# A decoder step whose first conditioning columns become features straight from fp32 weights

## The chip, the cores and the metric

The kernel runs on one core of a Trainium2 chip as a single program. The metric is the device time of one execution in microseconds (us); times of several executions are given by their median. TensorE (PE in the profile) multiplies matrices, and its weight loads stand apart as PEld. VectorE is DVE, ScalarE is ACT, GpSimd is POOL, and SyncE (SP) issues the transfers.

## What is computed

One layer of a hybrid decoder, for a prompt of 2048 tokens and for 64 sample tokens (8 sequences of 8), all in fp32. The part that matters here is its entry:

```python
ada = silu(c) @ w_ada + b_ada                    # c: 1 prompt row and 8 sample rows, w_ada: 1024 x 6144
sh_m, sc_m, g_m, sh_f, sc_f, g_f = split(ada, 6) # 1024 columns each
h = rmsnorm(x, norm_mix) * (1 + sc_m) + sh_m
proj = h @ w_in                                  # 1024 x 3584
# then retention and stick-breaking attention, w_out, and a gated MLP with a short convolution
```

Each of the six parts is a shift, a scale or a gate, and differs by row: row 0 of the nine conditioning rows belongs to the prompt, rows 1 to 8 to the eight sample sequences.

## The kernel before

An fp32 product is made from two fp32r numbers, high and low: `split` (line 173) copies the high part on ACT and subtracts for the low part on DVE, and three matmuls (`mm3`, lines 295 to 297) or, with a short left side, two, give the product. Weights arrive as `raw` tiles of 1 MB and are split into `whl` tiles, of which the pool has six buffers, that is three pairs.

The head (from line 1425) is all that runs before the first projection. It needs `coef[0]` (scale) and `coef[1]` (shift), which hold for each of the 1024 features the nine values of the conditioning rows, and `xT`, the first 512 prompt tokens and the 64 sample tokens, normalized and turned so that features lie on partitions. `modulate` (line 587) makes `acts` from both: `acts[0]` holds features 0 to 511, `acts[1]` the rest. Scale and shift are four blocks of 512 columns of `w_ada`: block 2 and block 0 are scale and shift of the lower half of the features, block 3 and block 1 those of the upper half.

- `prep` (line 466) applies silu to the nine rows and turns them into `s18`, high and low side by side.
- `ada` (line 505) takes a block: 2 MB in two loads, four splits, and sixteen matmuls at line 516, with `s18` as the weights and 512 columns of `w_ada` moving. The result, 18 rows of 512 columns, goes through ACT to `ar` (line 521), the bias is loaded into row 18, and four fp32 matmuls with the constant `fold` (line 551) add the high part, the low part and the bias and turn the columns onto partitions. DVE writes `coef` from there (lines 558 and 562).
- `raw_features` (line 569) does five tiles of x, four of 128 prompt rows and one of 64 sample rows: load, sum of squares on ACT (line 384), a short chain on POOL, scaling on DVE (line 576), eight PE transposes (line 580), and two evacuations to `xT`, one on DVE and one on ACT (line 584).
- `vectors` (line 477) loads small vectors as rows and turns them with one transpose (line 490).

The pool for the head holds three buffers for x, four for `raw`, and two for `ar`. A load that needs a buffer in use waits in SP's queue, and all that follows it in that queue waits with it. A scheduler orders each engine's instructions from the program's order; every engine then runs its own list strictly in order. After the head, `modulate` and the first two split column blocks of `w_in` let the projection begin: the matmuls of lines 295 to 297 on `d` and `z` with `act` and `whl`.

Of the kernel before, what the change touches and what calls it, by code (L numbers as in the profile page):

```python
# [5 lines left out]
F32 = mybir.dt.float32  # L6
# [3 lines left out]
ALU = mybir.AluOpType  # L10
# [3 lines left out]
P = 128  # L14
D = 1024
KT = D // P
SEQ = 2048
NB = 4
TB = SEQ // NB
NT = TB // P  # L20
DB = 8
DS = 8
NS = DB * DS
# [124 lines left out]
def body(tc, I, O):  # L148
    nc = tc.nc
    pe, dve, act, pool, sp = nc.tensor, nc.vector, nc.scalar, nc.gpsimd, nc.sync  # L150
# [3 lines left out]
    def T(pl, shape, dt, tag):  # L154
        count[0] += 1
        return pl.tile(shape, dt, tag=tag, name=f"{tag}_{count[0]}")

    def tt(eng, o, a, b, op):
        eng.tensor_tensor(o, a, b, op)  # L159
# [7 lines left out]
    def ld(o, i):  # L167
        dma(sp, o, i)
# [4 lines left out]
    def split(hi, lo, src, eng=dve):  # L173
        act.copy(hi, src)  # L174
        tt(eng, lo, src, f(hi), ALU.subtract)
# [83 lines left out]
    def pd():  # L259
        return T(psd, [P, 512], F32, "d")  # L260
# [17 lines left out]
    def w_rows(src, r0, n, c0, pl=None):  # L278
        for r in range(r0, r0 + n, 4):
            m = min(4, r0 + n - r)  # L280
            raw = T(pl or wraw, [P, 2048], F32, "raw").rearrange("p (a b) -> p a b", a=4)
            ld(
                raw[:, :m],
                src[r * P : (r + m) * P, c0 : c0 + 512].rearrange("(k p) c -> p k c", p=P),
            )
            yield r - r0, raw[:, :m]
# [179 lines left out]
    def prep(pl, kp):  # L466
        sg = T(pl, [P, D], F32, "hj")[:9]
        act.activation(sg, c9, AF.Sigmoid)
        tt(dve, c9, c9, sg, ALU.mult)
        ps = pz()  # L470
        for k in range(KT):
            pe.transpose(ps[:, k * 16 : k * 16 + 9], c9[:, k * P : (k + 1) * P], ident[:9, :9])
        s18 = T(kp, [P, KT, 18], F32R, "s18")
        split(s18[:, :, 0:9], s18[:, :, 9:18], ps[:, : KT * 16].rearrange("p (k s) -> p k s", s=16)[:, :, 0:9])
        return s18

    def vectors(pl):
        rows = T(pl, [108, P], F32, "vrows")
        for nme, o, n in (
            ("norm_mix", V_NM, 8), ("norm_ffn", V_NF, 8), ("conv_w", V_CW, 66),  # L480
            ("conv_b", V_CB, 22), ("sb_gn", V_SG, 4),
        ):
            src = I[nme][0]
            if nme == "conv_w":
                src = src.rearrange("j (a p) -> (j a) p", p=P)
            else:
                src = src.rearrange("(a p) -> a p", p=P)
            ld(rows[o : o + n, :], src)
        ps = pz()
        pe.transpose(ps[:, :108], rows, ident[:108, :108])  # L490
        dve.tensor_copy(vecs, ps[:, :108])

    def state_rows(pl):
        ps = pz()
# [71 lines left out]
            yield 0.9  # L566


    def raw_features(hp, xT):

        for i, o, n in TILES + [(NT, TB, NS)]:
            x = T(hp, [P, D], F32, "hx")
            ld(x[:n], xp[o : o + n, :] if i < NT else xs)
            junk = T(hp, [P, D], F32, "hj")
            r = row_rstd(x, [junk[:, :512], junk[:, 512:]], n)
            dve.tensor_scalar(x[:n], x[:n], r[:n, 0:1], None, ALU.mult)
            for kh in range(2):
                ps = pz()
                for k in range(4):
                    pe.transpose(  # L580
                        ps[:, k * n : (k + 1) * n], x[:n, (kh * 4 + k) * P : (kh * 4 + k + 1) * P], ident[:n, :n]
                    )
                src = ps[:, : 4 * n].rearrange("p (k t) -> p k t", k=4)
                (act.copy if kh else dve.tensor_copy)(xT[:, kh * 4 : kh * 4 + 4, o : o + n], src)
            yield
# [831 lines left out]
    def chain(*gens):  # L1417
        for g in gens:
            yield from g
# [3 lines left out]
    with tile_pool("in1", 2) as ip0:  # L1423
        ip = _Bufs(ip0, dict(xt=2, rot=1, hf=3, st=2, kf=2, vst=1, ar=1, s18=1, gnm=1))
        with tile_pool("head", 2) as hp0:
            hp = _Bufs(hp0, dict(hx=3, hj=1, xT=1, vrows=1, raw=4, ar=2))
            first = {2: list(w_rows(I["w_ada"][0], 0, KT, 1024, hp))}
            s18 = prep(hp, ip)
            xT = T(hp, [P, KT, TB + NS], F32, "xT")
            feats = raw_features(hp, xT)  # L1430
            vectors(hp)
            for n, _ in enumerate(ada(hp, s18, (2, 0, 3), first)):
                if n:
                    next(feats, None)
            for _ in ada(hp, s18, (1,), first):
                pass
            first_in[0, 0, SQ] = list(w_fm(w_in, SQ))
            modulate(xT, coef[0], coef[1], acts, range(4))
            modulate(xT, coef[0], coef[1], acts, range(4, 8))
            bb = T(cp, [P, HS], F32, "bb")  # L1440
            ld(bb, I["sb_bias"][0].partition_broadcast(P))
            nb = T(cp, [P, HS], F32, "nb")
            dve.tensor_scalar(nb, bb, -1.0, None, ALU.mult)
            sel4 = T(cp, [4, P], F32R, "sel4")
            dve.tensor_copy(sel4, cc("sel4", 4))
            gnm.append(T(ip, [P, 512], F32, "gnm"))
            ld(gnm[0], I["ret_gn"][0].partition_broadcast(P))
            state_rows(hp)
        c9_cm.__exit__(None, None, None)
        with tile_pool("dec", 2) as dp0:  # L1450
            dp = _Bufs(
                dp0,
                dict(smp=1, page=3, khl=2, vhl=3, aT=10, qsm=1, ksm=1, oT=1,
                     tm=1, sbsq=1, dm=1, dmh=1, ptab=1, sbc=1, dbias=1, m8n=1),
            )
            smp = T(dp, [P, KT, 2, NS], F32R, "smp")
            for kh in range(2):
                pool.tensor_copy(smp[:, kh * 4 : kh * 4 + 4], f(acts[kh][:, :, :, TB:]))
            ins = _Stream(
                chain(*[in_block(g, ip, smp) for g in range(NB)]), 650.0  # L1460
            )
            rest = _Stream(ada(ip, s18, (4, 5, 6, 7, 8, 9, 10, 11)), 60.0)
            side = _Stream(decode(dp), 490.0)
            _weave([ins, side, rest], side)
        with tile_pool("ret", 1) as rp0, tile_pool("att0", 2) as tp0:
            rp = _Bufs(rp0, dict(rmh=3, qT=2, kT=1, rv=2, rg=2, scd=2, km=1, on=3, S=2, bst=4, mv=2, nm=2, va=2))
            tp = _Bufs(tp0, dict(aq=1, abe=6, aom=2, ahl=4, o2=1, sbsq=1))
            ins.total, ins.got = 650.0 - ins.got, 0.0
            _weave([
                ins,  # L1470
                rest,
                _Stream(chain(retention_sample(rp), retention(rp)), 100.0),
                _Stream(attention([0], tp), 60),
            ])
# [92 lines left out]
```

## Time and profile before

| what | us |
|---|---|
| median of 3 runs | 3450.88 |
| lowest and highest of them | 3449.73, 3461.42 |
| the profiled execution | 3453.42 |
| its span, first to last instruction | 3451.7 |
| PE busy in the span | 3287.4 (95%) |
| DVE busy | 2288.9 (66%) |
| ACT busy | 1779.6 (52%) |
| POOL busy | 1018.7 (30%) |

The profile is one execution. In its timeline an entry is a start, a duration, the engine, the source line, the operation, and "out<-in"; instructions of one kind in a row are merged into one entry with their count, whose duration runs from the first start to the last end. An fp32 matmul that isn't a transpose shows as two records on PE. What stands in brackets is the idle time before an entry and what ended it. Where a window's granted clock of TensorE is given, 1.00 is 2.4 GHz and 0.50 is 1.2 GHz.

### The profile page before, as it was taken

How to read it: one execution, taken by the hardware profiler on the slowest of the kernel's cores; microseconds unless marked ns; L12 is line 12 of the kernel's file. 1: busy time of each engine (PE TensorE's matmuls, PEld its weight loads, DVE VectorE, ACT ScalarE, POOL GpSimd, SP SyncE). 2: the span in 40 equal slices, each digit the busy share in tenths (PEclk: the TensorE clock that was granted, in tenths of full speed). 3: DMA queues.
4: the chain of work that ended last, by engine and by line, in shares of the span. 5: the costliest groups of instructions: out<-in, count | busy, mean ns of one | idle time of the engine just before them, and what ended most of it. 6: DMA issues, size and time to landing. Idle time of an engine off the chain costs nothing. (4 is left out here: it accounts for less than half of the span.)

```text
span 3451.7 us, 49588 instructions
## 1 busy us (share of the span) xinstructions
PE 3287.4 (95%) x17111; PEld 2683.8 (78%) x17111; DVE 2288.9 (66%) x3258; ACT 1779.6 (52%) x3153; POOL 1018.7 (30%) x1898
## 2 busy tenths in 40 slices
PE   7998999999999989999998999999899999999998
PEld 5877777776677767877877788777677787799997
DVE  5466666665555567777777787876877775554545
ACT  5457566654544446555556555554655553433223
POOL 3012011101343233434334343333433323321113
PEclk8999999999999999999999999999999999999999
DMA  6766766666756773433454343335333334332221
GB/s 227 232 200 193 231 224 224 220 229 201 212 172 197 242 215 107 123 115 120 122 185 130 107 124 112 118 109 189 110 119 107 115 103 138 119 110 84 80 86 65
DMA packets 406232, 527.71 MB, mean 153 GB/s; under 512 B 27830, under 2 KB 244009, under 8 KB 405982
## 3 DMA queue, kind: packets, MB, share of 16 engines
q1 hardware_dynamic: 405982, 524.55, 48.4%
q8 instruction: 136, 2.23, 0.3%
q14 instruction: 114, 0.93, 0.1%
HBM read 442.47 MB, written 81.99 MB: 152 GB/s over the span
## 5 line engine op out<-in xcount | busy, mean ns | idle before, releaser
L159 DVE TENSOR_TENSOR whl<-raw,whl 128x1024 fp32r<-128x1024 f32 x456 | 572.9, 1260 | 557.5 <-ACT whl L174 552.2
L174 ACT CAST whl<-raw 128x1024 fp32r<-128x1024 f32 x456 | 477.1, 1050 | 901.7 <-PE d L296 636.4
L295 PE MATMUL d<-act,whl 128*128 128x512 f32 (+2 forms) x2016 | 740.3, 368 | 7.8 <-ACT act L424 7.0
L297 PE MATMUL d<-act,whl 128*128 128x512 f32 (+2 forms) x2016 | 736.0, 365 | 4.6 <-DVE whl L159 4.6
L296 PE MATMUL d<-act,whl 128*128 128x512 f32 (+2 forms) x2016 | 733.1, 364 | 3.1 <-POOL act L159 2.2
L295 PEld LDWEIGHTS d<-act,whl 128*128 128x128 f32 x2016 | 384.6, 191 | 67.9 <-ACT act L424 8.7
L297 PEld LDWEIGHTS d<-act,whl 128*128 128x128 f32 x2016 | 384.2, 191 | 64.8 <-DVE whl L159 5.9
L296 PEld LDWEIGHTS d<-act,whl 128*128 128x128 f32 x2016 | 385.4, 191 | 59.8 <-POOL act L159 2.6
L295 PE MATMUL d<-whl,ff 128*128 128x512 f32 x704 | 280.2, 398 | 0.0
L297 PE MATMUL d<-whl,ff 128*128 128x512 f32 x704 | 279.4, 397 | 0.0
L296 PE MATMUL d<-whl,ff 128*128 128x512 f32 x704 | 279.1, 396 | 0.0
L295 PE MATMUL d<-whl,act 128*128 128x512 f32 x640 | 258.0, 407 | 10.4 <-DVE hf L159 9.3
L296 PE MATMUL d<-whl,act 128*128 128x512 f32 x640 | 258.3, 404 | 0.1
L297 PE MATMUL d<-whl,act 128*128 128x512 f32 x640 | 257.1, 402 | 0.0
L1139 DVE TENSOR_TENSOR_SCAN aom<-aom,acy 128x512 f32<-128x512 f32 x192 | 251.6, 1310 | 3.6 <-ACT aom L1125 3.0
L159 DVE TENSOR_TENSOR abe<-abe,aom 128x512 f32<-128x512 f32 (+2 forms) x320 | 232.1, 725 | 27.0 <-POOL abe L1129 5.1
L1163 PE MATMUL acc<-ahl,avv 128*128 128x512 f32 (+3 forms) x640 | 226.4, 413 | 17.6 <-ACT ahl L174 9.9
L1125 ACT ACTIVATE aom<-z,nb 128x512 f32<-128x512 f32 (+2 forms) x320 | 201.4, 629 | 74.6 <-PE z L1122 58.1
L1122 PE MATMUL z<-akk,aq 128*128 128x512 f32 (+3 forms) x640 | 192.9, 377 | 12.0 <-DVE scd L159 5.8
L1126 ACT ACTIVATE abe<-z,bb 128x512 f32<-128x512 f32 (+2 forms) x320 | 200.1, 625 | 0.0
L159 DVE TENSOR_TENSOR ahl<-z,ahl 128x512 fp32r<-128x512 f32 (+1 forms) x320 | 191.4, 598 | 6.7 <-ACT ahl L174 6.4
L159 POOL TENSOR_TENSOR ff<-ff,hf 128x512 f32<-128x512 f32 (+1 forms) x101 | 159.4, 1600 | 105.3 <-DVE hf L159 91.5
(292 smaller groups left out, 6208.8 us busy)
## 6 DMA issues: line engine op xcount, KB each, us to landing
raw<-in_w_in SPq DMA_DIRECT2D x56, 1024.0 KB
raw<-in_w_up_gate SPq DMA_DIRECT2D x44, 1024.0 KB
raw<-in_w_up_val SPq DMA_DIRECT2D x44, 1024.0 KB
akk<-k SPq DMA_DIRECT2D x160, 256.0 KB
page<-in_cache_k_pages SPq DMA_DIRECT2D x128, 256.0 KB
page<-in_cache_v_pages SPq DMA_DIRECT2D x128, 256.0 KB
raw<-in_w_down SPq DMA_DIRECT2D x32, 1024.0 KB
raw<-in_w_ada SPq DMA_DIRECT2D x24, 1024.0 KB
```

The costliest lines, as they stand in the source:

```text
L159: eng.tensor_tensor(o, a, b, op)
L174: act.copy(hi, src)
L295: pe.matmul(ps, sh, mh, start=start, stop=False)
L296: pe.matmul(ps, sh, ml, start=False, stop=False)
L297: pe.matmul(ps, sl, mh, start=False, stop=stop)
L1122: pe.matmul(z[:, :n], qs[g, h][:, i * P : (i + 1) * P], kk[:, c, :n], start=c == 0, stop=c == 1)
L1125: act.activation(om[:, :n], z[:, :n], AF.Sigmoid, bias=nb[:, h : h + 1], scale=-SCALE)
L1126: act.activation(be[:, :n], z[:, :n], AF.Sigmoid, bias=bb[:, h : h + 1], scale=SCALE)
L1139: dve.tensor_tensor_scan(rv, rv, rv, init, ALU.mult, ALU.bypass)
L1163: pe.matmul(accs[0][:, cs], kv[u][1][:, kt, :], m[:, cs], start=(s == g and kt == 0 and c == 0), stop=(s == 0 and kt == NT - 1 and c == 1),)
```

## The change

Blocks 2 and 0 are computed another way, and the order of loads and of PE's work in the head is another. Blocks 3 and 1 keep the old way.

- `prep` also returns `s9`, the turned conditioning rows in plain fp32.
- `ada_features` is new. It takes 128 columns of the unsplit fp32 `raw` tile as the weights and nine columns of `s9` as the moving side, so that the result has features on partitions at once: 32 fp32 matmuls a block, which sum four row tiles each into one of two column groups of a PSUM tile. Two additions on DVE sum the groups and the bias, and a third operation makes the scale. The casts, the subtractions, the copy to `ar` and the `fold` matmuls of the two blocks are gone.
- The bias of all four blocks comes with the small vectors (`bvec`), as 16 more rows of the same transpose.
- All five tiles of x get a buffer of their own and are loaded right behind block 2; block 0 follows. Block 3 is loaded into the two buffers of `wraw`, which the first block of `w_in` uses next. Block 1 takes the buffers that block 2 leaves. `ar` has one buffer instead of two.
- `modulate` of features 0 to 511 is called between blocks 3 and 1.

The core of the diff:

```diff
     def prep(pl, kp):
...
-        split(s18[:, :, 0:9], s18[:, :, 9:18], ps[:, : KT * 16].rearrange("p (k s) -> p k s", s=16)[:, :, 0:9])
-        return s18
+        pv = ps[:, : KT * 16].rearrange("p (k s) -> p k s", s=16)[:, :, 0:9]
+        s9 = T(pl, [P, KT, 9], F32, "s9")
+        dve.tensor_copy(s9, pv)
+        split(s18[:, :, 0:9], s18[:, :, 9:18], s9)
+        return s9, s18
...
+    def ada_features(s9, bvec, j, raws):
+
+        ps = pd()
+        for k0, raw in raws:
+            for q in range(4):
+                o = (k0 + q) * 16
+                for k in range(4):
+                    pe.matmul(
+                        ps[:, o : o + 9], raw[:, k, q * P : (q + 1) * P], s9[:, k0 + k, :],
+                        start=k == 0, stop=k == 3,
+                    )
+            yield
+        kind, half = divmod(j, 2)
+        pv = ps[:, :128].rearrange("p (c q s) -> p c q s", c=2, s=16)[:, :, :, 0:9]
+        wide = lambda a, o: a[:, o : o + 4].unsqueeze(2).to_broadcast([P, 4, 9])
+        c = coef[1 - kind][:, half * 4 : half * 4 + 4, :]
+        tt(dve, c, pv[:, 0], wide(bvec, j * 4), ALU.add)
+        tt(dve, c, c, pv[:, 1], ALU.add)
+        if kind == 1:
+            dve.scalar_tensor_tensor(c, c, 1.0, wide(vecs, V_NM + half * 4), ALU.add, ALU.mult)
...
-            hp = _Bufs(hp0, dict(hx=3, hj=1, xT=1, vrows=1, raw=4, ar=2))
-            first = {2: list(w_rows(I["w_ada"][0], 0, KT, 1024, hp))}
-            s18 = prep(hp, ip)
+            hp = _Bufs(hp0, dict(hx=5, hj=1, xT=1, vrows=1, raw=4, ar=1, s9=1, bvec=1))
+            rows_of = lambda j, pl=hp: list(w_rows(I["w_ada"][0], 0, KT, j * 512, pl))
+            xrows = first_rows(hp)
+            first = {2: rows_of(2)}
+            rows = list(xrows)
+            first[0] = rows_of(0)
+            s9, s18 = prep(hp, ip)
             xT = T(hp, [P, KT, TB + NS], F32, "xT")
-            feats = raw_features(hp, xT)
-            vectors(hp)
-            for n, _ in enumerate(ada(hp, s18, (2, 0, 3), first)):
-                if n:
-                    next(feats, None)
+            bvec = vectors(hp)
+            first[3] = rows_of(3, wraw)
+            feats = raw_features(hp, xT, rows)
+            for _ in chain(ada_features(s9, bvec, 2, first.pop(2)), ada_features(s9, bvec, 0, first.pop(0))):
+                next(feats, None)
+            next(feats, None)
+            first[1] = rows_of(1)
+            for _ in ada(hp, s18, (3,), first):
+                pass
+            modulate(xT, coef[0], coef[1], acts, range(4))
             for _ in ada(hp, s18, (1,), first):
                 pass
             first_in[0, 0, SQ] = list(w_fm(w_in, SQ))
-            modulate(xT, coef[0], coef[1], acts, range(4))
             modulate(xT, coef[0], coef[1], acts, range(4, 8))
```

In the orders below a row is a source line, the operation, "out<-in" with buffer numbers, the shape, and how many such follow each other. PE's list near its end of the head, before the change: block 0's last matmuls (`d_332`), x tiles and `fold` matmuls stand by turns, and block 3 (`d_453`) follows the last x tile (`hx_427`, 64 sample rows).

```order
L516 MATMUL d_332<-whl_386,s_120_226 18x512
L516 MATMUL d_332<-whl_387,s_120_226 18x512
L580 MATMUL z_407<-con_171,hx_394 128x128 x4
L580 MATMUL z_413<-con_171,hx_394 128x128 x4
L551 MATMUL z_421<-con_171,ar_331 128x9 x4
```

PE's list now, from the turning of the conditioning rows on: `d_262` is block 2, `d_344` block 0, the `hx` tiles are the five of x, and `d_453` is block 3.

```order
L472 MATMUL z_231<-con_171,c_105_168 128x9 x8
L508 MATMUL d_262<-s_128_241,raw_210 128x9 x16
L508 MATMUL d_262<-s_128_241,raw_212 128x9 x16
L508 MATMUL d_344<-s_128_241,raw_224 128x9 x16
L508 MATMUL d_344<-s_128_241,raw_226 128x9 x16
L495 MATMUL z_253<-con_171,vrows_246 128x124
L613 MATMUL z_290<-con_171,hx_214 128x128 x4
L613 MATMUL z_296<-con_171,hx_214 128x128 x4
L613 MATMUL z_329<-con_171,hx_216 128x128 x4
```

All transposes of x, which stood between the matmuls of blocks 2 and 0, now stand behind both blocks; three more tiles and then block 3 follow.

DVE's list around the last evacuation of x (`xT_229<-z_440`, 64 sample rows) and block 3's first subtraction (`whl_457`), before:

```order
L584 COPY xT_229<-z_407 128x4x128
L558 COPY coef_108_174<-z_421 128x36
L576 TENSOR_SCALAR hx_427<-hx_427,rs_b_436 64x1024
L593 TENSOR_SCALAR xT_229<-xT_229,coef_107_173,coef_108_174 128x512 x2
L584 COPY xT_229<-z_440 128x4x64
L159 TENSOR_TENSOR whl_457<-raw_454,whl_456 128x1024
L159 TENSOR_TENSOR whl_465<-raw_454,whl_464 128x1024
```

The same place now (`z_436` is the last tile, `whl_455` block 3's first subtraction):

```order
L617 COPY xT_245<-z_372 128x4x128
L617 COPY xT_245<-z_411 128x4x128
L626 TENSOR_SCALAR xT_245<-xT_245,coef_107_173,coef_108_174 128x512
L617 COPY xT_245<-z_436 128x4x64
L159 TENSOR_TENSOR whl_455<-raw_258,whl_454 128x1024
L626 TENSOR_SCALAR xT_245<-xT_245,coef_107_173,coef_108_174 128x512
L159 TENSOR_TENSOR whl_463<-raw_258,whl_462 128x1024
```

Block 3's subtractions still stand behind the last evacuation of x, and one of the two modulating operations has moved behind it too.

SP's list before, from the head's last loads of `w_ada` on (`ar_498` is the bias of block 1):

```order
L165 DMA raw_500<-in_w_ada 128x4x512
L165 DMA raw_518<-in_w_ada 128x4x512
L165 DMA ar_498<-in_b_ada 1x512
L165 DMA raw_544<-in_w_in 128x8x256
L165 DMA bb_594<-in_sb_bias 128x8
L165 DMA gnm_600<-in_ret_gn 128x512
L165 DMA raw_603<-in_state_conv 16x1408
```

The same place now (`ar_452` is block 3's buffer of 19 rows, `ar_514` block 1's):

```order
L165 DMA raw_448<-in_w_ada 128x4x512
L165 DMA raw_450<-in_w_ada 128x4x512
L165 DMA ar_452<-in_b_ada 1x512
L165 DMA raw_556<-in_w_in 128x8x256
L165 DMA ar_514<-in_b_ada 1x512
L165 DMA bb_586<-in_sb_bias 128x8
L165 DMA gnm_592<-in_ret_gn 128x512
L165 DMA raw_595<-in_state_conv 16x1408
```

Both biases now stand here, and `ar_514` waits until block 3's `fold` matmuls have read the one buffer; the state of the convolution (`state_conv`) is issued behind it. From the second pair of projection blocks on, each engine's list is in the main the one of before; POOL's is the same throughout.

## Rows read from the trace of the kernel before

**Rows 1.** Busy time by stretch: stretch, PE, PEld, DVE, ACT, POOL, clock, DMA share, GB/s.

```profile
0.00:57.00 57.00, 37.34 (x147) 18.32 (x147) 33.44 (x39) 34.96 (x56) 18.16 (x35) 0.79 0.72 252
57.00:100.00 43.00, 43.00 (x318) 39.93 (x319) 22.11 (x31) 20.93 (x36) 8.72 (x11) 1.00 0.64 204
```

**Rows 2.** Timeline of PE in the head, from the conditioning rows to the projection.

```profile
6.78 1.02 PE L472 MATMUL z<-con,c 9*128 9x9 f32 x8 [6.78 <-DVE c L159]
10.32 4.01 PE L516 MATMUL d<-whl,s 128*18 128x512 f32 x10 [0.65 <-DVE whl L159]
14.17 0.26 PE L490 MATMUL z<-con,vrows 108*128 108x108 f32 x1
14.20 1.37 PE L516 MATMUL d<-whl,s 128*18 128x512 f32 x5
19.53 1.06 PE L580 MATMUL z<-con,hx 128*128 128x128 f32 x8 [1.75 <-DVE hx L576]
...
25.42 1.97 PE L580 MATMUL z<-con,hx 128*128 128x128 f32 x8 [0.17 <-DVE hx L576]
...
35.48 1.09 PE L580 MATMUL z<-con,hx 64*128 64x64 f32 x8 [1.04 <-DVE hx L576]
...
47.73 1.87 PE L551 MATMUL z<-con,ar 19*128 19x9 f32 x8 [0.24 <-ACT ar L521]
49.53 5.95 PE L516 MATMUL d<-whl,s 128*18 128x512 f32 x15
...
56.15 1.06 PE L551 MATMUL z<-con,ar 19*128 19x9 f32 x8 [0.40 <-ACT ar L521]
57.13 0.40 PE L297 MATMUL d<-act,whl 128*128 128x288 f32 x1
...
58.53 0.86 PE L500 MATMUL z<-con,raw 16*128 16x16 f32 x11
```

**Rows 3.** PE alone by stretch: stretch, busy time and records, granted clock, DMA share, GB/s.

```profile
20.80:27.20 6.40, 5.16 (x17) 0.50 0.81 276
27.60:34.00 6.40, 3.71 (x23) 1.00 1.03 364
47.70:49.50 1.80, 1.77 (x8) 0.50 0.97 333
49.50:54.40 4.90, 4.90 (x13) 0.50 0.54 197
54.80:60.00 5.20, 4.80 (x38) 1.00 0.00 0
```

**Rows 4.** Line 551 by source: shortest, median and longest record in ns.

```profile
L551 PE MATMUL z<-con,ar x64: 252/252/378, 16.7 to 571.2; 19*128 19x9 f32 x64
```

**Rows 5.** Timeline of PE much later: fp32 weights of 128 rows, two columns moving.

```profile
2888.16 0.95 PE L440 MATMUL z<-con,sbsq 128*128 128x2 f32 x8
```

**Rows 6.** DMA rate in forty slices of one us from the span's start.

```profile
GB/s 0 4 112 294 399 408 412 395 387 371 297 152 328 410 410 426 397 391 389 383 346 4 209 272 389 387 383 387 391 387 387 285 326 403 252 18 245 386 383 145
```

**Rows 7.** Timeline of DVE from the last evacuation of x to the upper half's shift.

```profile
34.47 0.20 DVE L558 COPY coef<-z 128x36 f32<-128x36 f32 x1 [0.81 <-PE z L551]
...
35.26 0.99 DVE L593 TENSOR_SCALAR xT<-xT,coef,coef 128x512 f32<-128x512 f32 x2
36.17 0.42 DVE L584 COPY xT<-z 128x256 f32<-128x256 f32 x1
36.52 1.22 DVE L159 TENSOR_TENSOR whl<-raw,whl 128x1024 fp32r<-128x1024 f32 x1
...
57.24 0.20 DVE L558 COPY coef<-z 128x36 f32<-128x36 f32 x1 [2.49 <-PE z L551]
```

**Rows 8.** Groups of instructions in the first 60 us: count, busy us, mean ns.

```profile
L159 DVE TENSOR_TENSOR whl<-raw,whl 128x1024 fp32r<-128x1024 f32 x18 | 23.4, 1322 | 2.7 <-ACT whl L174 2.0 <-DMA raw<-in_state_conv 0.8
L174 ACT CAST whl<-raw 128x1024 fp32r<-128x1024 f32 x18 | 18.5, 1043 | 2.1 <-PE d L516 1.7 <-DVE whl L159 0.4
```

More of the change, by code (lines that the diff above doesn't have):

```diff
@@ L473, in prep @@
         s18 = T(kp, [P, KT, 18], F32R, "s18")
-        split(s18[:, :, 0:9], s18[:, :, 9:18], ps[:, : KT * 16].rearrange("p (k s) -> p k s", s=16)[:, :, 0:9])
-        return s18
+        pv = ps[:, : KT * 16].rearrange("p (k s) -> p k s", s=16)[:, :, 0:9]
[3 more added lines that the diff above has]
+        return s9, s18
     def vectors(pl):
-        rows = T(pl, [108, P], F32, "vrows")
+        rows = T(pl, [124, P], F32, "vrows")
         for nme, o, n in (
             ("norm_mix", V_NM, 8), ("norm_ffn", V_NF, 8), ("conv_w", V_CW, 66),
-            ("conv_b", V_CB, 22), ("sb_gn", V_SG, 4),
+            ("conv_b", V_CB, 22), ("sb_gn", V_SG, 4), ("b_ada", 108, 16),
         ):
             src = I[nme][0]
-            if nme == "conv_w":
+            if nme == "b_ada":
+                src = src[: 4 * 512].rearrange("(a p) -> a p", p=P)
+            elif nme == "conv_w":
                 src = src.rearrange("j (a p) -> (j a) p", p=P)
@@ L489, in vectors @@
         ps = pz()
-        pe.transpose(ps[:, :108], rows, ident[:108, :108])
+        pe.transpose(ps[:, :124], rows, ident[:124, :124])
         dve.tensor_copy(vecs, ps[:, :108])
+        bvec = T(pl, [P, 16], F32, "bvec")
+        dve.tensor_copy(bvec, ps[:, 108:124])
+        return bvec
+    def ada_features(s9, bvec, j, raws):
[17 more added lines that the diff above has]
+            dve.scalar_tensor_tensor(c, c, 1.0, wide(vecs, V_NM + half * 4), ALU.add, ALU.mult)
     def state_rows(pl):
@@ L566, in ada, with first_rows @@
             yield 0.9
-    def raw_features(hp, xT):
+    def first_rows(hp):
         for i, o, n in TILES + [(NT, TB, NS)]:
@@ L573, in raw_features @@
             ld(x[:n], xp[o : o + n, :] if i < NT else xs)
+            yield x
+    def raw_features(hp, xT, rows):
+        for x, (i, o, n) in zip(rows, TILES + [(NT, TB, NS)]):
             junk = T(hp, [P, D], F32, "hj")
```

## The prediction

> **What bounds the kernel now.** I read the stretches first. From 57 us on PE has work without a gap, 43.00 of 43.00 us up to 100 us, while in the first 57 us it is busy for 37.34 [rows 1]. The lists of all engines are almost the same behind the head. So the question is by how much the moment at which PE runs through moves; that shift is carried to the end nearly one to one. In the timeline of PE this moment is 57.13 us, when the projection's matmuls run through behind the last fold matmuls [rows 2].
>
> What ends last ahead of it is read backwards. The upper half's shift is written by DVE at 57.24 us, after a chain of splits that begins at 36.52, right behind the last evacuation of x at 36.17 [rows 7]. That evacuation waits for the last transposes of x, which end at 35.48 + 1.09 = 36.57 us [rows 2]. So the head has two parts: up to the end of the x transposes at 36.57, and 20.7 us of chain from there to the shift. The second part is the same work in both kernels, eight splits of blocks 3 and 1 and those of w_in, at 1.04 us a cast and 1.32 us a subtraction [rows 8]. What the change moves is the first part.
>
> The clock needs care. The stretches give 1.00 for the first 20 us, yet line 516 takes 4.01 us for ten records at 10.32 and 1.37 us for five at 14.17 [rows 2]. The first is 0.40 each, as in the last stretch of the head, where fifteen take 5.95 us at a granted 0.50 [rows 2, 3]. So TensorE begins at 1.2 GHz and reaches 2.4 GHz only shortly before 14 us.
>
> **Loads.** Before, x tiles and weights wait for buffers, and the rate falls to 152 GB/s in the twelfth us and to 4 in the twenty-second [rows 6]. Now 2.46 MB (conditioning rows, constants, block 2) come first, as before; the slices add up to that shortly after 9 us. Then x (2.36 MB) and block 0 (2.10 MB) at about 395 GB/s take 11.3 us, so x is there at 15 us, the halves of block 0 at 17.7 and 20.4. Block 3 follows by about 26 us, block 1 by 31 us. Against before this removes waits. It gains only if something waits for loads, and the next part says that PE will be later than they are.
>
> **Features on PE.** Removed are, for blocks 2 and 0, eight casts (8 x 1.04 = 8.3 us of ACT), eight subtractions (8 x 1.32 = 10.6 us of DVE) and 32 matmuls of line 516. That work was done by 34.47 us, when DVE wrote the lower half's shift [rows 7], and it ran between the x tiles. Added are 64 fp32 matmuls, 128 records, each with new weights of 128 columns and nine columns moving. The nearest row is line 551, the same nine columns and the same fp32 weights of 128 columns, on 19 rows. Eight of its records take 1.87 us at the clock of 0.50 and 1.06 us at 1.00 [rows 2, 3]; less the last record's own 0.378 and 0.252 [rows 4] that is 0.213 and 0.115 us from one to the next. With weights of 128 rows line 440 has (0.95 - 0.25) / 7 = 0.10 at the full clock [rows 5], so the rows cost nothing more. A block is then 64 x 0.213 = 13.6 us at 1.2 GHz or 7.4 at 2.4.
>
> Which clock? PE starts on block 2 cold. At 47.73 us it runs eight records of line 551 and then, without a gap, fifteen of line 516, all at 0.50, up to 54.4 [rows 2, 3]. Ahead of the rise shortly before 14 us stood ten records of line 516 in 4.01 us; no row shows a rise with nothing but records of line 551 ahead of it. I take the clock of the nearest row, 1.2 GHz, for both blocks. Then PE starts at 7.80 us, the end of the conditioning transposes [rows 2], plus 0.3 for DVE's copy of s9, at 8.1; both blocks end at 8.1 + 27.3 = 35.4 us, and PE never waits for a load, since block 0 is there at 20.4 and block 2 is done at 21.8.
>
> **The x transposes behind them.** All forty now stand behind both blocks in PE's list. The scaled rows are ready long before (loaded by 15 us; ten squares on ACT and five scalings on DVE follow). First comes the transpose of the vectors, 0.26 us. Eight x records take 1.97 us at 0.50 and 1.06 at 1.00, the last eight 1.09 [rows 2]. Five tiles are 4 x 1.97 + 1.09 = 9.0 us cold, 4 x 1.06 + 1.06 = 5.3 warm. A row speaks for a rise on the way: the tile at 25.42 ran at 0.50, and the stretch from 27.6 is at 1.00 [rows 2, 3]. I take 7.3 us, so they end at 35.4 + 0.3 + 7.3 = 43.0 us, with bounds 41.0 and 44.7.
>
> The Trainium skill has a rule against such a rise: by "TensorE: Matmul & The Clock Gate", part 4 (PE-mode transpose), transposes don't count as PE being busy. The rise behind the tile at 25.42 us, with matmuls on either side, doesn't agree with it; by the rule the tiles would take 9.0 us and the sum would be 1.7 us higher.
>
> **The chain behind.** The end of the x transposes moves from 36.57 to 43.0, by +6.4 us. One of DVE's two modulating operations (0.99 us for two [rows 7]) now stands behind the last evacuation: +0.5. Against it, the fifteen matmuls that took 5.95 us at 0.50 would take 15 x 0.27 = 4.1 at full clock, from the five at 14.20 in 1.37 [rows 2]; if the dense transposes leave the clock up, up to 1.9 us come back. I take -0.4. Sum: +6.5 us; bounds +4.4 - 1.4 = +3.0 and +8.1 + 0.5 = +8.6. The five new DVE operations on 36 columns, two for the shift and three for the scale (some 0.2 us each, as the one at 34.47 [rows 7]) lie between evacuations.
>
> **Waits that the change adds.** w_in's first load waits for a buffer of block 3, which the second subtraction frees some 3 us into the chain, near 47 us; its split is needed ten us later. The bias of block 1 waits in SP's queue for block 3's fold matmuls, which ended at 47.73 + 1.87 = 49.6 before, now near 56. Behind it stands the convolution's state, whose transposes PE ran at 58.53 and will reach near 65 [rows 2]. Three issues of about half a us and two to three us to land leave about five us to spare. I cost both at nothing.
>
> **Rivals.**
> *Warm.* Nine-column records keep the clock up, or raise it near 14 us as before. Then a block costs 7.4 us, the second half of block 0 begins at 21.4 and ends at 25.1, the transposes take 5.3 and end at 30.7 instead of 36.57: -5.9, with +0.5 for the moved operation -5.4 us, about 3445.5. For it: PE is busy without a break. Against it: the 6.7 us from 47.7 to 54.4, busy and at 0.50 [rows 3]. In the Trainium skill the same page ("What's actually happening") says that the clock follows how busy PE has recently been; by that rule this rival is what happens, and only the rows named make me doubt it.
> *Dearer weights.* A record with weights of 128 rows costs, cold, what the cold x transposes do: 1.97 / 8 = 0.246 us. Then 128 of them take 31.5 us, 4.2 more, and the time is +10.7, about 3461.6. For it: line 440 was seen at full clock alone. It passes the bound of 0.5% (17 us) only from 0.295 us a record, 38 us for both blocks; no row is that high.
> *SP's queue.* If the convolution's state lands over seven us after its issue, PE stalls on it in the middle of the projection; each further us adds one. It would need over 17 us to land to reach the bound together with the forecast's shift.
> *The loads don't come ahead.* If x delays the first half of block 0 past 21.8 us, PE waits. From 9 us on that is 3.41 MB, so it would take a rate below 270 GB/s where the slices have 395 [rows 6]; what it cost would be the delay beyond 21.8, and I give it no chance of its own.
>
> **How the numbers follow.** The profiled execution took 3453.42 us, 1.7 more than its span, and the median of the runs is 3450.88, 2.5 lower. The sum is a difference, so it applies to either: 3459.9 against the profiled run, 3457.4 against the median, which I forecast. Chances: forecast 0.64, warm 0.18, dearer weights 0.10, SP's queue 0.03, something else 0.05. The forecast's own range is 3453.9 to 3459.5. To hold 8 in 10 the whole range takes in the warm case and the scatter of a median: 3444.5 to 3463. A measurement can tell 0.5% (17 us) from no change. Faster by more needs the x transposes to end before 20 us, and the warm case has them end at 31: 0.02. Slower by more: 0.05, from the queue, from dearer weights and the rest. Within: 0.93.
>
> **What would show it.** Right: in the changed profile, line 508 in one unbroken run from 8 to 35 us with records 0.21 us apart, the loads of block 0 long landed, the x transposes from 36 to 43, the first subtraction of block 3 near 43.5 and the projection running through near 63.5. Wrong: 0.115 us between records from 14 us on, PE waiting for block 0 near 18 us, and the projection running through near 52.

## The result and the profile after

Over twelve runs each, the changed kernel took 3469.08 us (3460.63 to 3474.82) and the kernel before, on the same chip, 3454.66 (3448.04 to 3462.45). The ratio is 1.0039, interval 1.0027 to 1.0050: about 13.5 us more, within half a per cent, and above the forecast range, which ended at 3463. The profiled execution took 3466.62 us, its span is 3464.9.

The timeline of PE in the head of the changed kernel, against [rows 2] (start, duration, line, count, and in brackets what was waited for; lines have moved: the features are 508, x transposes 613, the old way 545, fold 580, the convolution's state 529):

```profile
8.30 27.47 PE L508 MATMUL d<-s,raw 128*128 128x9 f32 x128 [0.33 <-DVE s L476]
35.62 0.45 PE L495 MATMUL z<-con,vrows 124*128 124x124 f32 x1
35.86 6.71 PE L613 MATMUL z<-con,hx 128*128 128x128 f32 x40
42.50 0.41 PE L545 MATMUL d<-whl,s 128*18 128x512 f32 x1
...
53.10 1.87 PE L580 MATMUL z<-con,ar 19*128 19x9 f32 x8
54.90 5.31 PE L545 MATMUL d<-whl,s 128*18 128x512 f32 x12
...
62.09 1.05 PE L580 MATMUL z<-con,ar 19*128 19x9 f32 x8
63.07 0.40 PE L296 MATMUL d<-act,whl 128*128 128x288 f32 x1
...
64.87 0.86 PE L529 MATMUL z<-con,raw 16*128 16x16 f32 x11
```

And DVE's first subtraction of block 3 and the upper half's shift, against 36.52 and 57.24 in [rows 7]:

```profile
42.88 1.21 DVE L159 TENSOR_TENSOR whl<-raw,whl 128x1024 fp32r<-128x1024 f32 x1
...
63.18 0.20 DVE L587 COPY coef<-z 128x36 f32<-128x36 f32 x1 [1.49 <-PE z L580]
```

The head came out as forecast. The 128 feature records run without a gap at 27.47 / 128 = 0.215 us each, the price at 1.2 GHz in [rows 2, 3]. They end at 35.77 us (forecast 35.4), the x transposes at 42.57 (43.0), the first subtraction is at 42.88 (43.5), and the projection runs through at 63.07 (63.5), 5.9 us later than before. The loads now follow each other nearly without a break; this is the DMA rate in slices of one us, against [rows 6], mostly between 380 and 420 GB/s, and over at 33 us:

```profile
GB/s 0 4 84 309 387 406 412 399 389 401 414 422 401 401 348 205 358 385 381 389 392 331 358 387 391 385 391 387 385 389 387 387 109 16 0 0 0 0 0 0
```

So what is new is behind the head. Aligned by DVE instructions that do the same work, the changed kernel is 5.4 us later than before at 100 us, 7.2 at 450, 11.4 at 650 and 13.3 at 800; it falls back to 10.1 at 2400 and is 13.5 at the end. Here are the stretches that answer to 100 to 900 us of the kernel before (stretch, its length, busy time and records of PE, PEld, DVE, ACT, POOL, granted clock, DMA share, GB/s), first of before, then of the changed kernel:

```profile
100.00:900.00 800.00, 757.91 (x4040) 601.95 (x4040) 486.37 (x736) 450.93 (x817) 112.64 (x242) 0.98 0.66 215
```

```profile
105.40:912.40 807.00, 766.35 (x4040) 607.81 (x4039) 485.99 (x736) 450.55 (x817) 113.94 (x242) 0.97 0.66 214
```

PE does the same 4040 records, and is idle for 42.1 us before and 40.7 after. It is busy for 8.4 us more: the granted clock is 0.97 instead of 0.98. In the clock records of the trace PE is at 1.2 GHz for 47.8 us of this stretch, and for 30.7 before. At half the clock, 17.1 us more of this cost half of that, 8.5 us.

### The profile page after: what moved, and what is told of

It is laid out like the page before. It is cut to its first block, busy times and chain, and to the rows that moved or that the text cites. A ratio compares the mean times of both kernels' runs of the same rounds, so it can differ in the third digit from the quotient of the medians.

```text
span 3464.9 us, 49716 instructions
## 1 busy us (share of the span) xinstructions
PE 3306.9 (95%) x17191; PEld 2710.6 (78%) x17191; DVE 2280.5 (66%) x3255; ACT 1770.2 (51%) x3143; POOL 1023.9 (30%) x1898
## 3 DMA queue, kind: packets, MB, share of 16 engines
q8 instruction: 136, 2.23, 0.3%
## 5 line engine op out<-in xcount | busy, mean ns | idle before, releaser
L159 DVE TENSOR_TENSOR whl<-raw,whl 128x1024 fp32r<-128x1024 f32 x448 | 563.2, 1260 | 558.6 <-ACT whl L174 541.7
L174 ACT CAST whl<-raw 128x1024 fp32r<-128x1024 f32 x448 | 468.8, 1050 | 902.6 <-PE d L296 640.1
L295 PE MATMUL d<-whl,act 128*128 128x512 f32 x640 | 260.3, 410 | 12.4 <-DVE hf L159 9.9
```

What stands on the lines that cost most here:

```text
L295: pe.matmul(ps, sh, mh, start=start, stop=False)
```

## The experiments

Each is given against the kernel before on the same chip, as a ratio with its interval; 0.0001 is 0.35 us. "Later at 100 us" is the shift of the head in the profile, by DVE instructions of the same work, against the profile of before.

**The two kernels again**, unchanged.

> The kernel before once more, with a second profile. It measures how far two executions of one program lie apart, and where. If the 7 us that the changed kernel lost behind the head (shift of its instructions +6 us at 63 us, +13 us at the end) were the scatter of single executions, this profile against the first one should show shifts of the same size, up and down by 3 to 7 us, in the stretch from 400 to 900 us, where the clock fell 7 times before and 11 times after. If they are the change's own, the two profiles of before should agree within 2 us everywhere. Ratio to before: 1.000 within 0.001 by either.

> The changed kernel once more, with a second profile. Both theories: 1.0039 again, and +6 us at the start of the projection. Scatter: the part behind the head adds another amount than 7 us in this execution, between 0 and 7. The change's own: it adds 7 us again, at the same places (450 to 800 us and 2930 to 3070 us).

> The changed kernel a third time, beside the three others. If its loss behind the head is scatter by which way the clock falls, the mean over three sets approaches what the head shows, +5 to +6 us; if it is the change's own, it stays at +10 to +13 us. In either case the part of the program from 100 us to the end has the same idle time of PE as before (133 us in the profiles so far).

Before again: 0.9995 [0.9983, 1.0008], 0.8 us earlier at 100 us. After again: 1.0029 [1.0016, 1.0042] and 1.0025 [1.0014, 1.0037], 3.8 us later at 100 us in both. So the change costs 8.6 to 13.5 us, of which the head accounts for four to five and a half. Some 5 to 8 us are left over, in three comparisons out of three.

**A delay of the head and nothing else**: the kernel before, with 16 fp32 matmuls more ahead of the last x tile's transposes.

```
+                if i == NT and kh == 0:
+                    for k in range(16):
+                        pe.matmul(ps[:, :9], ident, con[:, :9], start=True, stop=True)
```

> The kernel before, with a pure delay in its head: 16 fp32 matmuls of nine columns (a constant as weights, a result that the next transposes overwrite) stand in PE's list ahead of the last x tile's transposes, and nothing else differs in any engine's order. At 1.2 GHz they take 32 x 0.213 = 6.8 us, so the projection should run through 6.8 us later, near 63.9. If a shift of the head is carried one to one, the time is +6.8 us (ratio 1.002). If a later start of the projection costs more than itself further down, it is +12 to +15 us (1.004), as in the changed kernel. If the excess comes from what the changed kernel does to buffers and loads, this one shows +6.8 and the changed one stays at +13.5.

The 16 matmuls in the timeline, and PE in two stretches there (stretch, length, PE busy and records, granted clock, DMA share, GB/s):

```profile
34.29 4.20 PE L581 MATMUL z<-con 128*128 128x9 f32 x32
```

```profile
34.30:37.30 3.00, 3.00 (x28) 1.00 0.57 185
37.50:38.40 0.90, 0.90 (x5) 0.50 1.08 380
```

1.0021 [1.0008, 1.0033], that is 7.2 us; 3.1 later at 100 us, 4.2 at the end of its profile. The delay came out smaller than the 6.8 us expected, since here the records began at the full clock: the first 28 stand 0.112 us apart, the last ones 0.213. The clock fell at 37.4 us in the midst of them, with PE busy without a gap. A delay of the head does reach the end; left over are 4.1 us, and the interval allows anything from none to 8.

**Half of the feature matmuls left out**, so that their sums are incomplete:

```
-                for k in range(4):
+                for k in range(2):
...
-                        start=k == 0, stop=k == 3,
+                        start=k == 0, stop=k == 1,
```

> The changed kernel with half of its feature matmuls: of four row tiles two are left out in each sum, so scale and shift of the lower half of the features are incomplete. All orders are the same but for those 32 matmuls, 64 records of 0.213 us, 13.7 us. The features then end near 24 us (block 0 has landed by 20.5), the x transposes near 30, and the projection runs through near 51. If PE at 1.2 GHz is what the changed kernel pays, the time is 12 to 14 us below the changed kernel's, 0 to 2 us above that of before if the excess behind the head stays, and 6 us below before if it goes with the shift.

```profile
8.11 7.00 PE L508 MATMUL d<-s,raw 128*128 128x9 f32 x32 [0.33 <-DVE s L476]
19.33 7.00 PE L508 MATMUL d<-s,raw 128*128 128x9 f32 x32 [4.21 <-DMA raw<-in_w_ada]
26.18 0.45 PE L495 MATMUL z<-con,vrows 124*128 124x124 f32 x1
26.42 7.15 PE L613 MATMUL z<-con,hx 128*128 128x128 f32 x40
```

PE now waits 4.21 us for block 0: with half of the feature matmuls, the loads become the bound. The price per record stays at 0.219 us, and the head is 10.4 us earlier than in the changed kernel. Result: 0.9997 [0.9987, 1.0007], 5.0 earlier at 100 us. So of the head's gain only about a us is left at the end; here too 4.0 us are left over.

**The loads alone**: after's loads and buffers (but two buffers for `ar`, as before), all four blocks the old way.

```
-            for _ in chain(ada_features(s9, bvec, 2, first.pop(2)), ada_features(s9, bvec, 0, first.pop(0))):
+            for n, _ in enumerate(ada(hp, s18, (2, 0), first)):
...
```

> One part of the change alone: the loads and buffers of the changed kernel (x behind block 2, each tile in a buffer of its own; block 0 next; block 3 in the two buffers that w_in uses next; two buffers for ar), but all four blocks the old way, by splits and 512-column matmuls. Theory (the loss is 128 nine-column records at 1.2 GHz ahead of x's transposes): PE has 64 matmuls of at most 0.43 us (27.5 us in all, spread between the x tiles), DVE some 37 us of work from 8.5 on, so the projection should run through near 47 to 50 instead of 57, and the time be 7 to 10 us below before (ratio 0.997 to 0.998). Rival (the loads themselves, or what they do to the decode stage, cost the time): 5 us or more above before.

```profile
9.69 6.32 PE L545 MATMUL d<-whl,s 128*18 128x512 f32 x16 [1.84 <-DVE s L159]
21.68 0.61 PE L545 MATMUL d<-whl,s 128*18 128x512 f32 x1 [5.66 <-ACT whl L174]
```

1.0002 [0.9988, 1.0016]; 0.6 earlier at 100 us. The gain of 7 to 10 us that I had expected isn't there. With x loaded ahead of block 0, the first split of block 0 comes late, PE waits 5.66 us for it, and the chain of casts and subtractions sets the end of the head as before.

**One block of features, and features apart.** In e6_one, block 2 by features and block 0 the old way:

```
-            for _ in chain(ada_features(s9, bvec, 2, first.pop(2)), ada_features(s9, bvec, 0, first.pop(0))):
+            for _ in ada_features(s9, bvec, 2, first.pop(2)):
+                pass
+            for _ in ada(hp, s18, (0,), first):
...
```

In e7_between, the x transposes stand between the two blocks; block 0 takes a copy of s9 that depends on xT, which holds it back.

```
+            s9b = T(hp, [P, KT, 9], F32, "s9b")
+            dve.scalar_tensor_tensor(s9b, xT[:, :, TB : TB + 9], 0.0, s9, ALU.mult, ALU.add)
...
```

> The changed kernel with block 2 alone as features and block 0 the old way. PE: block 2's 64 records from 8.1 to 21.8, then dense matmuls between x tiles; block 0's splits run on ACT and DVE meanwhile. Theory: the projection runs through near 50 to 53, 4 to 7 us below before and 10 to 13 below the changed kernel, since half of the slow records lie where PE would wait for splits anyway. Rival (excess behind the head belongs to the new loads): 3 to 5 us less gain, so about the same as before.

> The changed kernel with x's transposes in PE's list between the two feature blocks (block 0's features read a copy of the conditioning rows that waits for the last x tile). Block 2 to 21.8 us, x to about 29, block 0 to about 43; DVE splits block 3 from 29 on, under block 0's records. Theory (both the place of x's transposes and the records' price set the head): the projection runs through near 57 to 60, 3 to 6 us earlier than in the changed kernel. If the place does not matter, near 62.

```profile
8.18 13.83 PE L508 MATMUL d<-s,raw 128*128 128x9 f32 x64 [0.33 <-DVE s L476]
...
32.29 13.26 PE L508 MATMUL d<-s9b,raw 128*128 128x9 f32 x64 [2.20 <-DVE s9b L1475]
```

e6_one: 1.0018 [1.0007, 1.0028], though 1.2 us earlier at 100 us. e7_between: 1.0047 [1.0034, 1.0061], 4.7 later at 100 us. Both missed what I expected. The price of the features is nearly the same in any order (13.83 and 13.26 us a block). The second block of e7_between began at the full clock, 0.112 us from record to record, behind a wait of 2.20 us; the clock fell at 32.9 us, after six records, and the rest are 0.213 apart. Left over behind the head are 7.4 us in e6_one and 11.5 in e7_between, against 4.8 to 8.1 in the changed kernel. So moving the features does not take the rest away.

**Where the split weights lie.** With eight splits less, the buffers of pool whl are taken in turn from another place on, so that behind the head each split weight has another address than before. e9 turns them in the kernel before by small copies, e10 turns them back in the changed kernel.

```
+            for _ in range(8):          (4 in the changed kernel)
+                pool.tensor_copy(T(whl, [P, 1024], F32R, "whl")[:, :9], con[:, :9])
```

> The kernel before, with eight small POOL copies of nine columns into buffers of the pool whl at the start of the head. They are read by nobody; what they do is to turn the pool's rotation, so that from w_in on every split weight stands at the SBUF address that it has in the changed kernel. Instructions and their order are otherwise as before. Theory A (the about 5 us that features cost behind the head hang on where the split weights come to lie): +4 to +6 us on the median, 3456 to 3458 beside a before of 3451.6, with the projection running through at 57 as before. Rival B (the place of the buffers is without effect; the excess comes with the features themselves or with the clock alone): 0 to +1.5 us.

> The changed kernel, with four such copies, so that from w_in on every split weight stands at the SBUF address that it has in the kernel before. Order otherwise as in the changed kernel. Theory A: only the shift of the head is left, +5 to +6 us, 3456.5 to 3457.5 beside a before of 3451.6. Rival B: as the changed kernel, +9 to +11 us, 3460.5 to 3462.5.

1.0006 [0.9997, 1.0015] and 1.0042 [1.0028, 1.0056]. Theory A of these two falls by e10: with the addresses of before the changed kernel is as slow as ever, 14.5 us [9.7, 19.3] over the kernel before, more than rival B's 9 to 11 too. e9 alone would not tell, since its 2.1 us [-1.0, 5.2] reach into the 4 to 6 of theory A.

**Where the instruction loads come.** Queue 8 loads instructions. Its group for the whole execution is the same before and after (packets, MB, share):

```profile
q8 instruction: 136, 2.23, 0.3%
```

That is 2.23 MB / 136 = 16.4 KB each, and from 310 to 540 us the packets come once in 20 to 31 us. Their place in the work goes with the length of PE's list in the head. PE has 17111 matmul records before and 17191 after, and as many weight loads; for 136 packets that is 252 to 253 a packet. Worked back to the time of before by DVE instructions of the same work, a packet starts at 365.6 us before and at 372.8 to 373.0 in the three profiles of the changed kernel. In e3_delay, with 16 fp32 matmuls more, it is at 359.2, and in e4_half, with 32 fewer than the changed kernel, at 384.2. In the DMA view of 371 to 380 us of the changed kernel (366 to 375 before, where q1 alone is listed):

```profile
q1 hardware_dynamic: 1819, 2.51, 80.1%
q8 instruction: 1, 0.02, 0.8%
q14 instruction: 1, 0.01, 0.4%
```

In that stretch PE waits for a page that it had in time before. First before, then the changed kernel:

```profile
373.91 0.60 PE L813 MATMUL z<-con,page 128*128 128x128 f32 x4
```

```profile
379.94 0.63 PE L846 MATMUL z<-con,page 128*128 128x128 f32 x4 [1.13 <-DMA page<-in_cache_k_pages]
...
514.68 0.91 PE L846 MATMUL z<-con,page 128*128 128x128 f32 x4 [1.83 <-DMA page<-in_cache_k_pages]
```

At 514.68 another such wait, and right behind it a fall of the clock (stretch, length, PE busy and records, granted clock, DMA share, GB/s):

```profile
507.00:514.60 7.60, 5.86 (x28) 1.00 0.85 292
515.00:518.40 3.40, 3.40 (x13) 0.51 0.29 92
518.50:522.00 3.50, 3.50 (x17) 1.00 0.21 72
```

The test is small fp32 matmuls of nine rows and columns that nobody reads, by which PE's list grows. The scheduler puts them all at the front of the list, where PE waits for the conditioning rows. 24 in the changed kernel bring the packets to where they are in the kernel before, 40 in the kernel before bring them to where the changed kernel has them, and 64 leave them where they were in either. That fits the counts: 64 such matmuls are 128 records on PE and 128 weight loads, about one packet's worth, and 40 in the kernel before make 17191 records, as many as the changed kernel has.

```
+                        for k in range(3):     (2 or 3 in before; 8 and 4 for 64)
+                            pe.matmul(pad[:9, :9], ident[:9, :9], con[:9, :9], start=True, stop=True)
```

> The changed kernel with 24 small fp32 matmuls (nine rows, nine columns, read by nobody) in PE's list, three ahead of the matmuls of each split of blocks 3 and 1, where PE waits for the split. What they do is to lengthen PE's list ahead of the projection, so that the 16 KB packets of queue 8 that load instructions come at the same places of the work as in the kernel before (near 365 and 509 us of it, where the changed kernel has them near 373 and 496). Theory A (the changed length of PE's list moves these packets, and they delay page loads that PE waits for; that is the excess behind the head): the waits for pages near 380 and 514 us are gone, and only the head's shift is left, +4.5 to +6.5 us, 3456 to 3458 beside a before of 3451.5. Rival B (the packets are without effect on the whole): as the changed kernel, +9 to +12 us, 3460.5 to 3463.5.

> The kernel before with 40 such matmuls, two ahead of the matmuls of each split of blocks 2 and 0 and three for blocks 3 and 1, so that the packets come where the changed kernel has them. They fill waits of PE; the head may end up to 1 us later. Theory A: the waits for pages near 380 and 514 us of the changed kernel turn up here, and the time is +4 to +7 us, 3455.5 to 3458.5 beside a before of 3451.5. Rival B: 0 to +1.5 us.

> The changed kernel with 64 of the small matmuls ahead of the conditioning transposes instead of 24. By the places seen so far (16 fp32 matmuls more moved the packets of queue 8 ahead by 5 to 6 us, 32 fewer back by 11, at a spacing of 21 us near 370 us), 64 move them by one whole spacing, so that they stand where the changed kernel has them. The small matmuls may end later than the conditioning transposes could start and put the head off by up to 1.5 us. Theory A (the place of the packets makes the excess): +9 to +12.5 us against before, with waits for pages near 380 and 514 us. Rival B (it is the early matmuls that took the excess away in the kernel with 24): +4 to +6.5 us.

> The changed kernel with 24 small matmuls once more, beside the one with 64 on the same chip. If the loss of the excess was no accident of one chip and hour: +3 to +6 us against before, and 5 to 7 less than with 64 by theory A, within 2 by rival B.

> The kernel before with 64 of them: the packets stand where the kernel before has them. With 40, the head was 2.8 us earlier in the profile, since the tile at 19 and those behind ran nearer to the full clock. Theory A: as the shift of the head, -3 to +1 us. Rival B, by which the place of the packets is without effect: the same, -3 to +1 us; what tells them apart here is only the difference to the kernel with 40, +3 to +6 less by A, none by B.

> The kernel before with 40 small matmuls once more: by theory A +1 to +4 us against before (the head's -2.8 and the excess of 4 to 7), by rival B -3 to 0 us.

The kernels by the place of the packet near 370 us (in time of before); "left over" is the whole less the head, in us. The last four are the other runs, which were not built for a place:

| kernel | packet | later at 100 us | whole, us [interval] | left over |
|---|---|---|---|---|
| e1, before again | 365 | -0.8 | -1.7 [-5.9, +2.8] | -0.9 |
| e9, before turned | 366 | -0.5 | +2.1 [-1.0, +5.2] | +2.6 |
| e15, before, 64 | 364 | +0.2 | +0.7 [-4.1, +5.5] | +0.5 |
| e11, after, 24 | 363 | +4.3 | +2.8 [-1.4, +6.9] | -1.5 |
| e14, after, 24 | 366 | +4.0 | +7.3 [+3.5, +11.4] | +3.3 |
| e12, before, 40 | 373 | -2.8 | -0.3 [-4.1, +3.1] | +2.5 |
| e16, before, 40 | 373 | +0.4 | +7.3 [+1.7, +12.4] | +6.9 |
| after | 373 | +5.4 | +13.5 [+9.3, +17.3] | +8.1 |
| e2, after again | 373 | +3.8 | +10.0 [+5.5, +14.5] | +6.2 |
| e8, after again | 373 | +3.8 | +8.6 [+4.8, +12.8] | +4.8 |
| e10, after turned | 373 | +5.2 | +14.5 [+9.7, +19.3] | +9.3 |
| e13, after, 64 | 373 | +4.9 | +14.5 [+9.0, +20.0] | +9.6 |
| e7, features apart | 373 | +4.7 | +16.2 [+11.7, +21.1] | +11.5 |
| e5, loads alone | 365 | -0.6 | +0.7 [-4.1, +5.5] | +1.3 |
| e4, half | 363 and 384 | -5.0 | -1.0 [-4.5, +2.4] | +4.0 |
| e3, delay | 359 and 381 | +3.1 | +7.2 [+2.8, +11.4] | +4.1 |
| e6, one block | 356 and 377 | -1.2 | +6.2 [+2.4, +9.7] | +7.4 |

The first five have a mean of 0.8 left over, the next eight of 7.4. e5, whose PE list is as long as that of before, goes with the first five. In e4, e3 and e6 the packets lie between the two places, and 4.0 to 7.4 us are left over. On the side of the changed kernel the test is clear: with 24 small matmuls it is some 7 us shorter than with 64 (e14 against e13 on one chip; in 60 of the 66 pairs of one execution of each, e13's is the longer), and 64, which run just as early and for longer, take nothing off. So it isn't early work on PE that helps. The sizes were missed by a little: e13 and e14 lie 1 to 2 us above what theory A gave them, e11 lies 1.7 below. On the side of the kernel before it isn't shown: e12 missed, with a head that came 2.8 us earlier than I had expected, e16 lies above its 1 to 4 us, and the intervals of e16 and e15 overlap.

The waits near 370 us go with the place in most profiles. PE at the same work in e14 and e13, near 370 us of before:

```profile
376.70 0.60 PE L853 MATMUL z<-con,page 128*128 128x128 f32 x4
```

```profile
377.04 0.63 PE L853 MATMUL z<-con,page 128*128 128x128 f32 x4 [0.90 <-DMA page<-in_cache_k_pages]
```

And near 500 us in e16, which is the kernel before but for its small matmuls:

```profile
504.37 0.63 PE L820 MATMUL z<-con,page 128*128 128x128 f32 x4 [1.69 <-DMA page<-in_cache_k_pages]
```

All eight kernels with a packet at 373 wait for that page near 500 us, by 0.90 to 2.47 us. Of the first five of the table only e1 does, by 0.80; of the last four e5 by 0.44 and e6 by 1.97, e3 and e4 not at all. What makes the page late there isn't shown: in the changed kernel the packet lay at 503.2 us and took 1.0, and the page was issued only at 508.6. The stretches of e14 and e13 that answer to 100 to 900 us follow, with 34.1 and 44.4 us at 1.2 GHz by the clock records:

```profile
104.00:903.40 799.40, 759.16 (x4041) 603.23 (x4040) 484.41 (x736) 450.18 (x817) 114.61 (x242) 0.98 0.67 216
```

```profile
104.90:907.20 802.30, 763.48 (x4040) 605.26 (x4040) 486.28 (x736) 450.35 (x817) 112.96 (x242) 0.97 0.66 215
```

In this pair the stretch is as long as before with the packets back in their place, 799.4 us against 800.0, and 802.3 with them in after's place. Single profiles don't bear that out for all: of the eight with the packet at 373, four have 807.0 to 808.3 us in this stretch (after, e7, e8, e10), and four have 794.8 to 802.3 (e12, e16, e2, e13); the first five of the table have 794.0 to 800.7. A profile is one execution, so the 7 us stand on the medians of the runs, and where in the program they arise isn't settled.

What stays open: how much of the 5 to 8 us are such waits, and how much falls of the clock behind them. All waits of PE for pages in this stretch make 7.7 us in the changed kernel, 6.5 before, and 3.9 in e13, so their sum doesn't explain it; nor do the waits at these two places, which e3 and e4 don't have. A fall costs half of its length, 1.7 us for one of 3.4 us as above, and a few more of them in 800 us would do. Over the whole program they come at some thirty places in the profiles, and which of them come differs between two profiles of one kernel. That a packet causes them isn't shown. The packets of queue 14, which load instructions too, were not tried.

## Why the prediction was right and wrong

- **What bounds the head, and the price of the features: right.** 0.215 us a record, where 0.213 was taken from line 551. The ends forecast for features, transposes, first subtraction and projection were off by 0.4 to 0.6 us. The weights of 128 rows cost nothing more, so the rival of dearer weights falls. The part of the chain behind the x transposes was forecast 0.1 us longer (+0.5 - 0.4) and is 0.1 shorter, 20.50 us against 20.56 before; but nothing came back from the clock there, as the -0.4 had it: it was at 0.50 again from 50.7 to 60.9, and the eight `fold` records at 53.10 took 1.87 us as before.
- **The warm rival: wrong, as taken.** PE was busy for 27.47 us without a gap on nine-column records, and the price stayed that of 1.2 GHz in every one. By the Trainium skill, "TensorE: Matmul & The Clock Gate", "What's actually happening", the clock follows how busy PE has recently been; for this kind of work the trace doesn't agree. Nor do the traces of e3_delay and e7_between, where nine-column records began at the full clock and it fell in the midst of them. The rise came on the way through the x transposes: forty records in 6.71 us, between the 9.0 of a cold run and the 5.3 of a warm one, with nothing but transposes behind the features: at 40.4 us the records went from 0.213 to 0.11 us apart. That speaks against the rule in part 4 (PE-mode transpose) of the same page of the Trainium skill, by which transposes don't count as PE being busy.
- **Waits costed at nothing: right.** PE never waits for block 0, though the loads come later than forecast: in e4_half the first half of block 0 is waited for until 19.33 us, where 17.7 was forecast. The convolution's state, the one at stake in SP's queue, is transposed at 64.87 us without a wait.
- **"That shift is carried to the end nearly one to one": wrong.** This is the step that failed. It costed the stretch behind the head at zero, since the lists of the engines are almost the same there. They are almost the same, but they don't run the same: 5 to 8 us were added behind the head in three sets of runs. They go with the length of PE's list in the head, which moves every later load of instructions: with 24 small matmuls more in it, 3.3 us and none were left over (e14, e11), with 64 more 9.6 (e13). By what way the loads cost this time stays open. The forecast had a shift of +6.5 from the head (measured +5.4) and nothing besides.
- **The level: too low.** The median of before on which the forecast was built came from three runs, 3450.88; twelve had 3454.66. Of the 11.7 us between forecast and result this is 3.8. The level, the rest behind the head (8.1) and the head (-1.1) make 10.8; the other 0.9 is that the two medians lie 14.4 us apart, and the ratio gives 13.5. With the right level the forecast would still have been 7.9 us too low.
- **Within 0.5%: right**, and slower, as the sign of the sum said.

The change puts 27.5 us on PE ahead of the x transposes in place of work on ACT and DVE that lay between the x tiles. e4_half shows what would come next if the features cost half as much: PE waits 4.21 us for block 0's load, and the head gains 5.0 us against before.

## What to carry to other kernels

The nine-column fp32 matmuls cost the same with weights of 19 rows and of 128, 0.213 us a record at 1.2 GHz. Here 27.5 us of them brought no rise of the clock, and twice it fell while they ran: cost them at 1.2 GHz. When PE is nearly full, a change in the length of its list shifts loads of instructions all the way behind it; in the changed kernel some 7 us of 3450 came and went with that. Before you explain a difference of 0.2%, pad the list so that these loads stand where they stood, and see whether it stays.

## What the runs showed of the hardware

- Whether PE waits for a 256 KB page near 370 us goes with the place of a 16 KB load of instructions: five of the eight profiles with the packet at 373, between the page's issue and its use, have a wait of 0.89 to 1.16 us, two have 0.21 and 0.24, and one waits 1.22 us there for DVE; the five with the packet at 363 to 366, ahead of the issue, have none. That the packet delays the page is the likely reading; it isn't shown. In the Trainium skill, "Runtime: NRT & Kernel Launch", "Instruction fetch mechanics", the list is fetched in 16 KiB blocks by a DMA queue of its own, at a cost that is mostly hidden. The size agrees (2.23 MB in 136 packets). No row shows PE waiting for instructions either.
- Nine-column fp32 records don't hold the full clock here: in e3_delay it fell from 1.00 to 0.50 at 37.4 us, with nothing but such records on PE since 34.29 and no gap.
- Forty small matmuls between 4.5 and 6.7 us, in PE's idle time, made the head of the kernel before 2.8 us earlier in one profile (e12) and 0.4 later in the other (e16). It is no gain that could be relied on.
- Executions of one kernel on one chip scatter by some 20 us (3441.91 to 3461.60 for the kernel before, 33 of them). Twelve against thirty-three of them leave an interval of about 0.12% on either side.
